# Four groups of residual transposes at the end of an output projection gathered into one group, one product pair later

## The chip, the cores and the metric

One core of one Trainium2 chip runs the whole kernel. The metric is device microseconds for one execution. The kernel before takes 525.51 us (median of 3 runs, 525.22 to 525.74). Traces and engine names: PE is TensorE's matrix product, PEld its loading of the stationary operand, DVE is VectorE, ACT is ScalarE, POOL is GpSimd, SP is SyncE.

## The reference

One layer of an encoder on a residual `x` of 512 positions by 1024, in fp32:

```
h = RMSNorm(x);  [xr|gate|q|k|v] = h @ W_in
y_rnn  = (rg_lru_fwd(conv(xr)) + rg_lru_bwd(conv(xr))) * gelu(gate)
y_attn = dilated_attention(q, k, v)
x = x + concat(RMSNorm(y_rnn), RMSNorm(y_attn)) @ W_out
h = RMSNorm(x)
x = x + relu(h @ W_up)^2 @ W_down
out = RMSNorm(x)
```

The change lies where `x + ... @ W_out` ends and `h @ W_up` begins. The up projection needs the new residual with the model dimension on the partitions, so the residual is transposed there.

## The kernel before, in words

**Products.** Each fp32 operand is split into a high part and a low part (an ACT copy gives the high part, a DVE subtraction the low one). `mm3` (L311) then issues three products for one tile: high by high (L312), high by low (L313), low by high (L314). The first argument of `mm3` is the stationary operand. Weight chunks of 128x1024 are streamed: `conv_hi(i)` (L240) makes `whi` of chunk `i` on ACT, `conv_lo(i)` (L261, the subtraction at L269) makes `wlo` on DVE. Both run about three chunks ahead of PE.

**Order.** On PE, ACT, DVE and POOL the program order written in the kernel is the order of execution (`tc.manual_schedule`, L107). Nothing is moved behind another by a planner on these four engines. SP's queue of loads is planned outside the attention part.

**End of the output projection.** The attention half of `W_out` is multiplied as seven block products (`OSEQ`, L62: 11, s2, s3, s4, 21, s1, 22), each of four pairs `i` = 0 to 3, where pair `i` is `tt, k = i // 2, i % 2` (L1259 to L1266). One pair is one `mm3`. After `k == 1` the DVE instruction of `wo_x` (L1202, recorded at L1208) adds the product to the residual and writes a quarter of `x1n`. Block s1 writes `x1n[2,1]` and `x1n[3,1]`; block 22 writes `x1n[0,1]` and `x1n[1,1]`; so the right half of the new residual is complete only after the last pair of 22. The left half (`x1n[*,0]`) comes from blocks 21 and s4. What else is issued after each pair stands in the table `BES` (L1248 to L1258).

**Transposes.** `h2_t(k, tag)` (L1211) handles column block `k` of the residual: four PE transposes of 128x128 into one PSUM bank named `pxt` (L1218), then two ACT copies out of it: `h2h` (L1219) and `hm` (L1221). `h2_l(k)` (L1224) makes `h2l` on DVE. Blocks 0 to 3 read the left half and are spread over the pairs of s1 and 22, one group of four transposes each. Blocks 4 to 7 read the right half and are issued together, 16 transposes, after `k == 0` of the first three tiles of the up projection (L1531 to L1541). `pxt` uses the PSUM tags `gs` and `et`, two banks each; blocks 0 to 3 use `gs` only.

**Up projection, first three tiles.** For `k` = 0 to 7 and `i` = 0 to 2, PE multiplies chunk `c0 + i` by `h2h[k]`, `h2l[k]` into `pu`. The chunks are `C_WA+7`, `C_WA+8` and `C_WA+9`; their `conv_lo` stand in `BES` (after pair 3 of 21, pair 3 of s1 and pair 2 of 22).

The lines that the change and the prediction touch are `BES["s1"]` and `BES["22"]` (L1257, L1258), `h2_t` (L1211), `h2_l` (L1223), `wo_x` (L1202) and the start of the up projection (L1529 to L1541):

```
for k in range(KD):
    if k == 1:
        for j in range(4, 8):
            h2_t(j, "gs" if j < 6 else "et")
            h2_l(j)
    for i in range(start):
        mm3(pu[i], wk(c0 + i, k), h2k(k), k == 0, k == KD - 1)
```

Of the kernel before, what the change touches and what calls it, by code (L numbers as in the profile page):

```python
# [98 lines left out]
def hybrid_kernel(ctx: ExitStack, tc, xw0, xw, xn, w_in, w_v, w_out, w_up, w_dn, gates, vecs, bias, fg, out):  # L99
# [13 lines left out]
    def g_(name, dt=FT, shape=(P, S)):  # L113
        return work.tile(list(shape), dt, name=name, tag="g", bufs=NG)
# [4 lines left out]
    def ps_(name, tag):  # L119
        return psum.tile([P, S], FT, name=name, tag=tag, bufs={"pj": 4, "gs": 2, "et": 2}[tag])  # L120

    def f(t):
        return t.bitcast(FT)
# [4 lines left out]
    def vec(n, i):  # L128
        return vt[:, VEC[n] + i:VEC[n] + i + 1]
# [74 lines left out]
    C_G, C_V, C_QK, C_WO, C_WA, C_UP = 4, 8, 12, 20, 24, 31  # L204
# [3 lines left out]
    def ublock(h, b, f):  # L208
        return w_up[h * HF + f + {"11": 0, "12": 1, "21": 2, "22": 3}[b]]
# [11 lines left out]
    def wblock(h, b, q):  # L221
        return w_dn[h, int(b[1]) - 1, (int(b[0]) - 1) * NQ + q]
# [3 lines left out]
    def emit_dma():  # L226
        if plain:
            i = plain.popleft()
            r = stream.tile([P, 1024], FT, name="wraw", tag="wraw", bufs=3)
            nc.sync.dma_start(r, source(chunks[i]))  # L230
            raws[i] = r
# [29 lines left out]
    def conv_lo(i):  # L261
        if i < len(chunks):
            i = swap.get(i, i)
            r = raws.pop(i)
            if i in remade:
                splits[i] += (remade.pop(i),)
                return
            lo = stream.tile([P, 1024], FR, name="wlo", tag="wlo", bufs=4)
            nc.vector.tensor_tensor(lo, r, f(splits[i][0]), op=OP.subtract)  # L269
            splits[i] += (lo,)  # L270
            c = chunks[i]
            if isinstance(c, tuple) and c[0] == "o":
                return
            if isinstance(c, tuple) and len(c) == 4:
                h, kind, f0 = c[:3]
                if kind == "t1" and cq[h, f0, "t2"] not in raws:
                    nc.gpsimd.dma_start(r, ublock(h, "22", f0), accum_op=OP.add)
                    raws[cq[h, f0, "t2"]] = r
                elif kind == "22":
                    t = raws[cq[h, f0, "t3"]]  # L280
                    nc.vector.tensor_tensor(t, t, r, op=OP.add)
                elif kind in ("t2", "21"):
                    held[kind] = r
                    if len(held) == 2:
                        t = held.pop("t2")
                        nc.vector.tensor_tensor(t, t, held.pop("21"), op=OP.add)
                        raws[cq[h, f0, "t4"]] = t
                        emit_dma()
                if kind in ("11", "22"):
                    emit_dma()  # L290
            elif isinstance(c, tuple) and c[1][0] == "s":
                nxt = {"s1": ("s2", "22"), "s2": ("s4", "21")}.get(c[1])
                if nxt:
                    nc.gpsimd.dma_start(r, wblock(c[0], nxt[1], c[2]), accum_op=OP.add)
                    raws[cd_[c[0]] + {"s2": 2 * NQ + 2 * c[2], "s4": 6 * NQ + c[2]}[nxt[0]]] = r
            elif i not in (C_WO + 2, C_WO + 3):
                emit_dma()
# [492 lines left out]
    et, en, zs = {}, {}, {}  # L790
# [103 lines left out]
    def o_src(n, k):  # L894
        return at[k][:, tl] if n == "11" else osum[n, k]
# [4 lines left out]
    def o_lo(n, k):  # L900
        hi, lo = osp[n]
        c = slice(k * TH, (k + 1) * TH)
        nc.vector.tensor_tensor(lo[:, c], o_src(n, k), f(hi)[:, c], op=OP.subtract)
# [307 lines left out]
    def h2_t(k, tag):  # L1211
        if not hb:
            hb["h"] = big.tile([P, KD, S], FR, name="h2h", tag="bigB")
            hb["l"] = [t[:, j, :] for c in ("bigC", "bigD") for t in (big.tile([P, KD // 2, S], FR, name="h2l", tag=c),) for j in range(KD // 2)]
        pt = ps_("pxt", tag)
        n, j = k // 4, k % 4
        for tt in range(4):
            nc.tensor.transpose(pt[:, tt * P:(tt + 1) * P], x1n[tt, n][:, j * P:(j + 1) * P], ident)  # L1218
        act(hb["h"][:, k, :], pt, AF.Copy, scale=vec("mg", k))  # L1219
        hm[k] = g_("hm")  # L1220
        act(hm[k], pt, AF.Copy, scale=vec("mg", k))  # L1221

    def h2_l(k):  # L1223
        nc.vector.tensor_tensor(hb["l"][k], hm[k], f(hb["h"])[:, k, :], op=OP.subtract)  # L1224
# [20 lines left out]
    def cv(j):  # L1245
        return {0: lambda: conv_hi(C_WA + j), 3: lambda: conv_lo(C_WA + j)}

    BES = {w: cv(i + 3) for i, w in enumerate(OSEQ)}  # L1248
# [5 lines left out]
    BES["s3"][3] = lambda: (conv_lo(C_WA + 5), st["wo"](3))  # L1254
    BES["s4"].update({1: lambda: (o_lo("s1", 0), o_sum("22", 1)), 2: lambda: o_hi("22", 1)})
    BES["21"].update({1: lambda: o_lo("s1", 1), 3: lambda: conv_lo(C_WA + 7)})
    BES["s1"].update({1: lambda: (o_lo("22", 0), o_lo("22", 1), h2_t(0, "gs")), 2: lambda: h2_t(1, "gs"), 3: lambda: (conv_lo(C_WA + 8), h2_l(0))})  # L1257
    BES["22"].update({1: lambda: (h2_t(2, "gs"), h2_l(1)), 2: lambda: (h2_t(3, "gs"), conv_lo(C_WA + 9)), 3: lambda: (h2_l(2), h2_l(3))})  # L1258
    for w in OSEQ:  # L1259
        for i in range(4):  # L1260
            tt, k = i // 2, i % 2
# [260 lines left out]
    for half in range(2):  # L1522
# [6 lines left out]
        if half == 0:  # L1529
            start = 3  # L1530
            pu = [ps_("pu", "pj") for _ in range(start)]  # L1531
# [7 lines that stand above are left out]
                    if i == 0:  # L1539
                        feed(c0, k)  # L1540
                if k in (2, 3, 4, 5):  # L1541
                    h_sums(k - 2)
                if k == 6:
                    x1_sq(0, 0)
                if k in (5, 7):
                    h_hi("t1", k // 7)
                    h_lo("t1", k // 7)
            conv_hi(c0 + 4)
            conv_lo(c0 + 4)
            for i in (0, 1):  # L1550
                up_evac(i, pu[i])
            conv_hi(c0 + 5)
            conv_lo(c0 + 5)
            up_evac(2, pu[2])
# [262 lines left out]
```

## Time and profile before

| what | value |
|---|---|
| time, median of 3 runs | 525.51 us (525.22 to 525.74) |
| profiled execution, span from first to last instruction | 523.7 us, 8216 instructions |
| profiled execution's own time | the page gives its span only; the median lies 1.8 us above that span |
| PE busy | 517.1 us (99%), 3021 products |
| DVE busy | 430.4 us (82%) |
| ACT busy | 352.2 us (67%) |
| chain that ended last | PE 99% |
| mean granted TensorE clock | 0.999 |

A busy time of PE includes modelled ends of pipelined products, so a product is shown with 0.39 us where the next one starts 0.23 us later. The chain of waits removes that overlap: there each product of 512 columns counts 0.23 us. The timeline merges neighbouring instructions of one kind into one row; its bracket gives the idle time of the engine before the instruction and what ended it.

### The profile page before, as it was taken

What the parts mean: (1) busy time and instruction counts of PE and PEld (TensorE: products, weight loads), DVE (VectorE), ACT (ScalarE), POOL (GpSimd) and SP (SyncE); (2) the same over time, 40 slices, a digit from 0 to 9 for tenths busy, and PEclk for the clock granted to TensorE, in tenths of its full rate; (3) what the DMA queues carried; (4) which work ended last, traced back from release to release, by engine and by line L of the source; (5) the groups of instructions that cost most, each with busy time, mean ns of one, the idle gap of its engine ahead of it and who ended that gap; (6) DMA issues with size and microseconds to landing.
All of it is one profiled execution on the core that took longest, in us unless ns stands there. A gap on an engine that the chain in (4) does not pass through costs nothing.

```text
span 523.7 us, 8216 instructions
## 1 busy us (share of the span) xinstructions
PE 517.1 (99%) x3021; PEld 444.3 (85%) x3021; DVE 430.4 (82%) x668; ACT 352.2 (67%) x570; POOL 65.3 (12%) x89
## 2 busy tenths in 40 slices
PE   9999999999999999999999999999999999999995
PEld 8867888778777788899999888889999999888884
DVE  6899986788886898898789987789766978986885
ACT  7579946667857857586578666565667577655655
POOL 0173000000000321001300312001100300131000
PEclk9999999999999999999999999999999999999999
DMA  7636555266796499947595899976986497799704
GB/s 288 208 99 196 161 160 180 83 191 199 190 294 197 115 196 247 353 134 195 139 223 143 213 273 281 306 271 161 300 256 168 117 224 210 157 289 257 195 1 161
DMA packets 40329, 105.15 MB, mean 201 GB/s; under 512 B 5056, under 2 KB 13376, under 8 KB 40288
## 3 DMA queue, kind: packets, MB, share of 16 engines
q1 hardware_dynamic: 32448, 78.10, 44.5%
q0 software_dynamic: 7696, 26.32, 27.3%
q8 instruction: 24, 0.39, 0.3%
q10 hardware_dynamic: 144, 0.20, 0.1%
q14 instruction: 17, 0.14, 0.1%
HBM read 95.59 MB, written 4.29 MB: 191 GB/s over the span
## 4 chain that ended last, share of the span: by engine, by line
PE 99%; DVE 0%; issue 0%; DVEq 0%; ACT 0%; ACTq 0%
PE pu L314 10%; PE pu L312 10%; PE pu L313 10%; PE pd L314 10%; PE pd L312 10%; PE pd L313 10%; PE pqk L312 3%; PE pqk L314 3%; PE pqk L313 3%; PE pwo L312 3%; PE pwo L314 3%; PE pwo L313 3%; PE pav L942 2%; PE pt L842 2%; PE ps L806 2%; PE pp L312 1%
## 5 line engine op out<-in xcount | busy, mean ns | idle before, releaser
L269 DVE TENSOR_TENSOR wlo<-wraw,whi 128x1024 fp32r<-128x1024 f32 x71 | 86.6, 1220 | 24.0 <-ACT whi L247 23.9
L247 ACT ACTIVATE whi<-wraw 128x1024 fp32r<-128x1024 f32 x67 | 70.8, 1057 | 37.4 <-PE pd L314 18.4
L313 PE MATMUL pd<-wlo,ah 128*128 128x512 f32 (+1 forms) x195 | 75.2, 386 | 0.0
L312 PE MATMUL pd<-whi,ah 128*128 128x512 f32 (+1 forms) x195 | 75.2, 386 | 0.0
L314 PE MATMUL pd<-whi,al 128*128 128x512 f32 (+1 forms) x195 | 75.2, 386 | 0.0
L313 PE MATMUL pu<-hl,whi 128*128 128x256 f32 x224 | 63.4, 283 | 0.0
L314 PE MATMUL pu<-hh,wlo 128*128 128x256 f32 x224 | 63.4, 283 | 0.0
L312 PE MATMUL pu<-hh,whi 128*128 128x256 f32 x224 | 63.4, 283 | 0.0
L312 PE MATMUL pu<-h2h,whi 128*128 128x256 f32 (+1 forms) x200 | 60.1, 300 | 0.0
L313 PE MATMUL pu<-h2l,whi 128*128 128x256 f32 (+1 forms) x200 | 60.0, 300 | 0.0
L314 PE MATMUL pu<-h2h,wlo 128*128 128x256 f32 (+1 forms) x200 | 60.0, 300 | 0.0
L269 DVE TENSOR_TENSOR wlo<-tw,whi 128x1024 fp32r<-128x1024 f32 x37 | 45.2, 1221 | 17.7 <-ACT whi L247 17.7
L247 ACT ACTIVATE whi<-tw 128x1024 fp32r<-128x1024 f32 x38 | 40.1, 1058 | 24.9 <-PE pd L314 6.3
L312 PEld LDWEIGHTS pu<-hh,whi 128*128 128x128 f32 x224 | 43.0, 192 | 0.0
L313 PEld LDWEIGHTS pu<-hl,whi 128*128 128x128 f32 x224 | 43.0, 192 | 0.0
L314 PEld LDWEIGHTS pu<-hh,wlo 128*128 128x128 f32 x224 | 43.0, 192 | 0.0
L313 PEld LDWEIGHTS pd<-wlo,ah 128*128 128x128 f32 x195 | 36.6, 188 | 7.4
L312 PEld LDWEIGHTS pd<-whi,ah 128*128 128x128 f32 x195 | 36.6, 188 | 7.3
L314 PEld LDWEIGHTS pd<-whi,al 128*128 128x128 f32 x195 | 36.6, 188 | 7.4
L247 ACT ACTIVATE whi<-ts 128x1024 fp32r<-128x1024 f32 x24 | 25.4, 1060 | 25.2 <-PE pd L314 16.4
L313 PEld LDWEIGHTS pu<-h2l,whi 128*128 128x128 f32 x200 | 38.3, 191 | 1.3
L314 PEld LDWEIGHTS pu<-h2h,wlo 128*128 128x128 f32 x200 | 38.3, 191 | 1.3
(280 smaller groups left out, 1220.1 us busy)
## 6 DMA issues: line engine op xcount, KB each, us to landing
wraw<-in_w_up_dram SPq DMA_DIRECT2D x25, 512.0 KB, 4.8
ts<-in_w_dn_dram POOLq DMA_DIRECT2D x24, 512.0 KB, 13.5
wraw<-in_w_dn_dram SPq DMA_DIRECT2D x24, 512.0 KB, 8.7
tw<-in_w_up_dram SPq DMA_DIRECT2D x15, 512.0 KB, 6.7
tw<-in_w_up_dram POOLq DMA_DIRECT2D x15, 512.0 KB, 7.5
wraw<-in_w_in_dram SPq DMA_DIRECT2D x13, 512.0 KB, 4.3
ts<-in_w_dn_dram SPq DMA_DIRECT2D x8, 512.0 KB, 9.0
tw<-in_w_dn_dram SPq DMA_DIRECT2D x8, 512.0 KB, 7.0
```

Of the source, the lines that this page charges most:

```text
L247: act(hi, raws[i], AF.Copy)
L269: nc.vector.tensor_tensor(lo, r, f(splits[i][0]), op=OP.subtract)
L312: nc.tensor.matmul(o, lhsT=a[0], rhs=b[0], start=bool(first), stop=False, skip_group_check=on)
L313: nc.tensor.matmul(o, lhsT=a[0], rhs=b[1], start=False, stop=False, skip_group_check=on)
L314: nc.tensor.matmul(o, lhsT=a[1], rhs=b[0], start=False, stop=bool(last), skip_group_check=on)
L806: nc.tensor.matmul(psq[p, u][e][:, :NK], lhsT=qs_[p, a][r, P * qt:P * qt + P], rhs=kks[p][r, b, w:w + NK], start=i == 0, stop=i == 2)
L842: nc.tensor.transpose(pt[:, i * P:(i + 1) * P], en[h][qt][:, k:k + P], ident)
L942: nc.tensor.matmul(pav[p][a, co], lhsT=vs[:, jt, h * DH:(h + 1) * DH], rhs=et[h, jt][:, ci], start=jt == 0 and i == 0, stop=jt == 3 and i ...
```

## The change

The body of `h2_t` is cut into a PE part (`h2_pe`, the four transposes) and an ACT part (`h2_ev`, the two copies). In the table `BES`, the four groups of transposes that stood after pair 1 of s1, pair 2 of s1, pair 1 of 22 and pair 2 of 22 become one group of 16 after pair 2 of s1. Blocks 0 and 1 stay in the tag `gs`; blocks 2 and 3 take the tag `et`, so that the group has four PSUM banks. The copies of blocks 0 and 1 stand in ACT's order after pair 2 of s1, those of blocks 2 and 3 keep their places after pairs 1 and 2 of 22. The order of DVE's instructions is not changed.

```
+        h2_pe(k, tag)
+        h2_ev(k)
+    pxt = {}
+    def h2_pe(k, tag):
+        pt = pxt[k] = ps_("pxt", tag)
         n, j = k // 4, k % 4
         for tt in range(4):
             nc.tensor.transpose(pt[:, tt * P:(tt + 1) * P], x1n[tt, n][:, j * P:(j + 1) * P], ident)
+    def h2_ev(k):
+        pt = pxt.pop(k)
         act(hb["h"][:, k, :], pt, AF.Copy, scale=vec("mg", k))
         hm[k] = g_("hm")
         act(hm[k], pt, AF.Copy, scale=vec("mg", k))
...
-    BES["s1"].update({1: lambda: (o_lo("22", 0), o_lo("22", 1), h2_t(0, "gs")), 2: lambda: h2_t(1, "gs"), 3: lambda: (conv_lo(C_WA + 8), h2_l(0))})
-    BES["22"].update({1: lambda: (h2_t(2, "gs"), h2_l(1)), 2: lambda: (h2_t(3, "gs"), conv_lo(C_WA + 9)), 3: lambda: (h2_l(2), h2_l(3))})
+    BES["s1"].update({1: lambda: (o_lo("22", 0), o_lo("22", 1)), 2: lambda: (h2_t(0, "gs"), h2_t(1, "gs"), h2_pe(2, "et"), h2_pe(3, "et")), 3: lambda: (conv_lo(C_WA + 8), h2_l(0))})
+    BES["22"].update({1: lambda: (h2_ev(2), h2_l(1)), 2: lambda: (h2_ev(3), conv_lo(C_WA + 9)), 3: lambda: (h2_l(2), h2_l(3))})
```

## Rows read from the trace of the kernel before

**Rows 1.** The page, part 1: busy time, share of the span, instructions.

```profile
PE 517.1 (99%) x3021; PEld 444.3 (85%) x3021; DVE 430.4 (82%) x668; ACT 352.2 (67%) x570; POOL 65.3 (12%) x89
```

**Rows 2.** Chain that ended last, from 205 us to the end: shares by line.

```profile
by line: PE pu L314 16.8%; PE pu L312 16.8%; PE pu L313 16.8%; PE pd L314 15.9%; PE pd L312 15.8%; PE pd L313 15.8%; DVE x1n L1482 0.2%; DVE x1n L1473 0.2%; DVE scr L1483 0.1%; DVE x1n L1475 0.1%; DVE tw L1493 0.1%; issue 0.1%; DVEq L1813 0
```

**Rows 3.** Waits from 192 to 212 us: engine, line, releaser: total us, times, longest.

```profile
DVE h2l L1224 <- ACT hm L1221: 2.1, 4, 0.7
...
DVE x1n L1208 <- PE pwo L314: 0.3, 1, 0.3
PEld pxt L1218 <- DVE x1n L1208: 0.2, 1, 0.2
```

**Rows 4.** Chain that ended last, 194 to 204 us: start, us, what.

```profile
194.50 0.24 PE pwo L314
194.73 0.44 PE pxt L1218 x4
...
196.77 0.24 PE pwo L314
...
199.53 0.44 PE pxt L1218 x4
...
200.43 0.23 PE pwo L314
...
202.49 0.23 PE pu L314
202.71 1.79 PE pxt L1218 x16
```

**Rows 5.** Timeline of DVE, 195 to 203 us: start, us, instruction [idle before].

```profile
195.99 0.75 DVE L903 TENSOR_TENSOR ol<-osum,oh 128x256 fp32r<-128x256 f32 x2
197.05 0.75 DVE L1208 SCALAR_TENSOR_TENSOR x1n<-pwo,nrc,x 128x512 f32<-128x512 f32 x1 [0.31 <-PE pwo L314]
197.71 1.21 DVE L269 TENSOR_TENSOR wlo<-wraw,whi 128x1024 fp32r<-128x1024 f32 x1
198.85 0.69 DVE L1224 TENSOR_TENSOR h2l<-hm,h2h 128x512 fp32r<-128x512 f32 x1
...
200.71 1.22 DVE L269 TENSOR_TENSOR wlo<-wraw,whi 128x1024 fp32r<-128x1024 f32 x1
201.84 0.74 DVE L1208 SCALAR_TENSOR_TENSOR x1n<-pwo,nrc,x 128x512 f32<-128x512 f32 x1
```

**Rows 6.** Timeline of PEld, 200 to 205 us.

```profile
200.50 0.19 PEld L313 LDWEIGHTS pu<-h2l,whi 128*128 128x128 f32 x1
...
202.10 0.19 PEld L314 LDWEIGHTS pu<-h2h,wlo 128*128 128x128 f32 x1
202.33 0.14 PEld L1218 LDWEIGHTS pxt<-ident,x1n 128*128 128x128 f32 x1
202.64 1.62 PEld L1218 LDWEIGHTS pxt<-ident,x1n 128*128 128x128 f32 x15 [0.17 <-DVE x1n L1208]
204.23 0.19 PEld L312 LDWEIGHTS pu<-h2h,whi 128*128 128x128 f32 x1
```

**Rows 7.** Timeline of ACT, 195 to 199 us.

```profile
195.21 0.69 ACT L1219 ACTIVATE h2h<-pxt,vt 128x512 fp32r<-128x512 f32 x1 [0.69 <-PE pxt L1218]
...
197.50 1.08 ACT L247 ACTIVATE whi<-wraw 128x1024 fp32r<-128x1024 f32 x1
```

**Rows 8.** Chain that ended last, in the attention: groups of six transposes.

```profile
117.98 0.81 PE pt L842 x6
121.53 0.66 PE pt L842 x6
```

**Rows 9.** Busy time by stretch: us, PE, PEld, DVE, ACT, POOL (instructions), PEclk, DMA share, GB/s.

```profile
201.00:203.00 2.00, 2.00 (x12) 1.59 (x11) 2.00 (x3) 0.29 (x1) 0.00 (x0) 1.00 1.03 219
...
518.00:520.00 2.00, 0.00 (x0) 0.00 (x0) 1.85 (x8) 0.96 (x3) 0.00 (x0) 1.00 0.59 151
520.00:523.70 3.70, 0.00 (x0) 0.00 (x0) 0.19 (x1) 0.13 (x1) 0.00 (x0) 0.81 0.40 142
```

More of the change, by code (lines that the diff above doesn't have):

```diff
@@ L1214, in h2_t @@
             hb["l"] = [t[:, j, :] for c in ("bigC", "bigD") for t in (big.tile([P, KD // 2, S], FR, name="h2l", tag=c),) for j in range(KD // 2)]
-        pt = ps_("pxt", tag)
+        h2_pe(k, tag)
[3 more added lines that the diff above has]
+        pt = pxt[k] = ps_("pxt", tag)
         n, j = k // 4, k % 4
```

## The prediction, made before the changed kernel was run

> **What bounds the kernel now.** I read the busy times first. TensorE is busy 99% of the span [rows 1], so a microsecond added to PE anywhere is a microsecond of the result unless PE waits later for something else. The chain from 205 us to the end answers that: it consists of the products of `pu` and `pd` and a last piece of DVE work of about 1% [rows 2]. No wait of PE is left there that could swallow a delay, so what the stage around the change gains or loses reaches the end in full. The question is thus only when PE comes out of that stage.
>
> Then I read the waits of the stage. Two count. VectorE waits 0.31 us for a product before one `x1n` instruction, and PE's loader waits 0.17 us for another `x1n` [rows 3, 5, 6]. The timeline of DVE shows that these two belong together. At 197.05 DVE begins `x1n[3,1]`, which had to wait for pair 3 of block s1 (the product at 196.77 of [rows 4]). From there DVE runs without a gap: `wlo` of `C_WA+8`, `h2l[0]`, `x1n[0,1]`, `h2l[1]`, `wlo` of `C_WA+9` and `x1n[1,1]`, which ends at 201.84 + 0.74 = 202.58 [rows 5]. The second of PE's 16 transposes loads at 202.64, 0.06 after that [rows 6]. So in this stage DVE is the bound: PE -> `x1n[3,1]` -> six DVE instructions back to back -> PE. PE arrives at the second transpose only slightly too early.
>
> **The change part by part: the groups.** Removed: four groups of four transposes, 0.44 us each (the first and the last of four are shown) [rows 4], 1.76 together. Added: one group of 16. The trace has such a group, blocks 4 to 7, with 1.79 us in the chain [rows 4], but that holds the wait. Without it: 15 loads go from 202.64 to the next product's load at 204.23 [rows 6], 1.59 / 15 = 0.106 each, so 16 take 1.70. Bounds: 1.62 (1.79 less the whole 0.17), and 2.16 at the dearest transposes of the trace (0.81 / 6 = 0.135 each; the cheap kind of the same group is 0.66 / 6 = 0.11) [rows 8]. I take 1.70, since it is the same instruction with the same tiles. PE alone would therefore win 1.76 - 1.70 = 0.06 us. A group pays nearly nothing for being a group of its own: 0.11 per transpose in a group of four, 0.106 in one of 16.
>
> **The place.** Before, two groups (0.88) lay ahead of the end of s1's pair 3: one after pair 1, one after pair 2. After the change the whole group of 16 does: 1.70. So pair 3 of s1 ends 1.70 - 0.88 = 0.82 later. DVE was already waiting there: its work before it ends at 195.99 + 0.75 = 196.74 [rows 5], so no slack is left, and `x1n[3,1]` begins at 197.05 + 0.82 = 197.87. The wait of DVE grows from 0.31 to about 1.13. Behind it in DVE's order stand the six instructions named above. None of them is moved by the diff, and each was started as the last one ended, so all slip by 0.82: `h2l[0]` ends at 198.85 + 0.69 + 0.82 = 200.36, `wlo` of `C_WA+9` at 200.71 + 1.22 + 0.82 = 202.75, `x1n[1,1]` at 203.40.
>
> **Who waits for them.** After pair 3 of s1, PE has no transposes left in block 22, so it makes the 0.88 of the two later groups good and reaches the up projection at -0.06 against before. There:
> - `h2l[0]` is needed at the load at 200.50 - 0.06 = 200.44 [rows 6], 0.08 after its end. Just in time; a few hundredths late would be covered by the next two.
> - `wlo` of `C_WA+9` is needed by the last product of `k == 0`, whose load stood at 202.10 [rows 6], now 202.04. It is there at 202.75 plus 0.06: a wait of about 0.75 that the trace of before does not have.
> - `x1n[1,1]` is needed by the second transpose of block 4. Before, that loaded at 202.64; now it can at 202.64 + 0.82 = 203.46.
>
> The last two do not add up. From the load of that product to the load of the second transpose PE needs about 0.45 (202.10 to 202.64 less the 0.09 that the wait cost beyond the usual spacing), and DVE takes 0.65 from the end of `wlo` to the end of `x1n[1,1]`; so the later one decides. PE leaves the stage 0.82 later than before, although its own work shrank by 0.06.
>
> **What costs nothing.** ACT's copies of block 0 begin 0.68 later, one pair (195.21 to about 195.9) [rows 7]; the four copies of blocks 0 and 1 push `whi` of `C_WA+9` from 197.50 to about 198.2, where it takes 1.08, and it is wanted by DVE at 200.71 + 0.82 = 201.5 and by PE at about 201.6 (two products before the load at 202.10). That is a cover of over 2 us. Copies of blocks 2 and 3 don't wait for PE any more; `h2h[2]` is wanted after the second set of transposes only. The new banks (`et`) were last read by `wo_x` of s4, two blocks of products earlier; blocks 6 and 7 take them again near 204, after the copies. Loads on SP follow `conv_lo` and slip with it by 0.8 us, three chunks ahead of their use. If that cover were gone it would show as a wait of PE, of which there is none after 205 now [rows 2].
>
> **Sum.** 0.82 on a span of 523.7 gives 524.5. The median of the runs lies 1.8 above the profiled span, so 525.51 + 0.82 = 526.3 us. With the group at 1.62 it is +0.74 (526.25), at 2.16 it is +1.28 (526.8).
>
> [...] The granted clock is 1.00 in the stretch with the group of 16 and its wait, and stays 1.00 from 518 to 520 us, where PE does nothing; only the last 3.7 us show 0.81 [rows 9]. [...]
>
> **Rivals.** *A gain.* If DVE made up the delay, the 0.06 of PE and the 0.09 of the old wait remain: -0.06 to -0.15, 525.4. For it: PE is the bound of the whole, and the group's work does shrink. Against it: the chain of DVE has no gap from 197.05 to 202.58, and `x1n[3,1]` already waits for PE [rows 5]. It would need 0.8 us of idle DVE in that stretch. [...]
>
> *Slower beyond doubt.* The group of 16 that now lies ahead of DVE's wait costs as much per transpose as the dear groups of the attention, 0.135 instead of 0.106 [rows 8]. Then pair 3 of s1 is 2.16 - 0.88 = 1.28 late, and 526.8 comes out. For it: the group switches to banks of another tag and ACT reads two of them meanwhile. Against it: the group of 16 in the same stage had the same mixture. It decides (over 0.2%, 1.05 us) from a group of 1.93 us on.
>
> [...]
>
> **How the numbers follow.** The forecast, DVE's chain slipping by 0.82, gets 0.73; the gain 0.09; the dear group 0.15; the clock 0.03. A difference of 0.2% (1.05 us) is about what a measurement of this kernel can tell from no change. The forecast's +0.82 is inside it, with about 0.04 of its own chance beyond; with the two slow rivals that makes 0.21 slower. The gain is inside it too, and only 0.02 is left for faster. Same: 0.77. The range goes from 525.5 (taking in part of the gain) to 526.9 (the dear group).
>
> **What would show it.** DVE's wait before `x1n[3,1]` at 1.0 to 1.2 us instead of 0.31; no wait among the six that follow; a new wait of PE's loader for `wlo` of about 0.7 us and one for `x1n` of 0.2 to 0.5; the 16 transposes of blocks 4 to 7 beginning their second load near 203.5; everything after that later by the same 0.8. The first group of 16 in the chain with 1.7. I am wrong if PE's loader shows no wait there, if the group of 16 is far from 1.7, or if the 0.8 is given back before the end.

## The result, and the profile after

The changed kernel takes 525.91 us (median of 21 runs, 525.37 to 526.43) against 525.22 for the kernel before in the same sessions (21 runs, 524.64 to 525.98). The medians differ by 0.69 us. The ratio is 1.0015, with a 95% interval of 1.001 to 1.0021: on 525.22 that is slower by 0.79 us, between 0.53 and 1.10.

The profiled span is 524.0 us, with 525.76 for that execution, against 523.7 before. That difference of 0.3 is not the loss: the stage began 0.56 us earlier in the profile after (pair 1 of s1 ends at 194.17, before at 194.73). Nearly all of that arises at the very start of the kernel, which the change doesn't touch: in the chain, nine PE instructions that write `pxr` (L453, from 4.52 us on) take 3.35 us in the profile before and 2.82 in the one after. So stages are compared here and not spans. I measure the stage from the end of pair 1 of s1 to the end of the second set of 16 transposes, both in the chain that ended last. Before it runs from 194.73 to 202.71 + 1.79 = 204.50 [rows 4], 9.77 us.

The chain of the changed kernel over the same stretch (start, us, what):

```profile
193.94 0.23 PE pwo L314
...
194.62 0.23 PE pwo L314
194.86 1.75 PE pxt L1224 x16
...
197.06 0.25 PE pwo L314
197.31 0.03 issue
197.34 0.04 DVE x1n L1208
...
198.01 0.75 DVE wlo L269
...
199.14 0.68 DVE h2l L1233
199.82 0.66 DVE x1n L1208
200.48 0.60 DVE h2l L1233
201.08 1.14 DVE wlo L269
202.22 0.67 DVE x1n L1208
202.89 0.04 issue
202.93 1.86 PE pxt L1224 x15
```

The stage goes from 193.94 + 0.23 = 194.17 to 202.93 + 1.86 = 204.79: 10.62 us, 0.85 more. What the reader is to see is that the chain leaves PE here. Before, it ran through products and transposes alone [rows 4]. Now it goes over to DVE with `x1n[3,1]` at 197.34 and comes back to PE only at 202.93, with the six DVE instructions that the prediction named. The rest of the kernel is unchanged: 523.7 - 204.50 = 319.2 before, 524.0 - 204.79 = 319.2 after.

The waits of the changed kernel from 192 to 213 us (engine, line, releaser: total us, times, longest) answer to [rows 3]:

```profile
DVE x1n L1208 <- PE pwo L314: 1.2, 1, 1.2
PEld pu L314 <- DVE wlo L269: 0.8, 1, 0.8
PE pu L314 <- DVE wlo L269: 0.4, 1, 0.4
PEld pxt L1224 <- DVE x1n L1208: 0.4, 1, 0.4
```

DVE's wait grew from 0.3 to 1.2, PE's loader has a wait for `wlo` that was not there, and its wait for `x1n` doubled.

The timeline of DVE after, answering to [rows 5]:

```profile
195.43 0.75 DVE L903 TENSOR_TENSOR ol<-osum,oh 128x256 fp32r<-128x256 f32 x2
197.34 0.75 DVE L1208 SCALAR_TENSOR_TENSOR x1n<-pwo,nrc,x 128x512 f32<-128x512 f32 x1 [1.16 <-PE pwo L314]
198.01 1.21 DVE L269 TENSOR_TENSOR wlo<-wraw,whi 128x1024 fp32r<-128x1024 f32 x1
199.14 0.68 DVE L1233 TENSOR_TENSOR h2l<-hm,h2h 128x512 fp32r<-128x512 f32 x1
199.74 0.74 DVE L1208 SCALAR_TENSOR_TENSOR x1n<-pwo,nrc,x 128x512 f32<-128x512 f32 x1
200.40 0.68 DVE L1233 TENSOR_TENSOR h2l<-hm,h2h 128x512 fp32r<-128x512 f32 x1
201.00 1.22 DVE L269 TENSOR_TENSOR wlo<-wraw,whi 128x1024 fp32r<-128x1024 f32 x1
202.14 0.74 DVE L1208 SCALAR_TENSOR_TENSOR x1n<-pwo,nrc,x 128x512 f32<-128x512 f32 x1
```

The two rows of before that [rows 5] leaves out, for the comparison:

```profile
199.45 0.74 DVE L1208 SCALAR_TENSOR_TENSOR x1n<-pwo,nrc,x 128x512 f32<-128x512 f32 x1
200.11 0.68 DVE L1224 TENSOR_TENSOR h2l<-hm,h2h 128x512 fp32r<-128x512 f32 x1
```

One wait in front, then no bracket until the last row, before as after: counted from the end of pair 1 of s1, `x1n[3,1]` begins 0.85 us later (3.17 for 2.32) and `x1n[1,1]` ends 0.86 later (8.71 for 7.85). The timeline of PE's loader, answering to [rows 6], shows where it arrives:

```profile
202.27 0.19 PEld L314 LDWEIGHTS pu<-h2h,wlo 128*128 128x128 f32 x1 [0.83 <-DVE wlo L269]
202.40 0.14 PEld L1224 LDWEIGHTS pxt<-ident,x1n 128*128 128x128 f32 x1
202.93 1.62 PEld L1224 LDWEIGHTS pxt<-ident,x1n 128*128 128x128 f32 x15 [0.39 <-DVE x1n L1208]
```

`wlo` ends on DVE at 201.00 + 1.22 = 202.22 and its load begins at 202.27; `x1n[1,1]` ends at 202.88 and the load of the second transpose begins at 202.93.

The clock stayed up through both waits and the transposes (us, PE, PEld, DVE, ACT, POOL, then PEclk, DMA share, GB/s):

```profile
201.00:203.00 2.00, 1.55 (x7) 0.72 (x6) 2.00 (x4) 0.03 (x1) 0.00 (x0) 1.00 1.07 225
203.00:205.00 2.00, 2.00 (x17) 1.96 (x18) 1.26 (x3) 1.48 (x3) 0.00 (x0) 1.00 1.03 272
```

### The profile page after: what moved, and what is told of

Read it like the earlier page. It is cut to its first block, busy times and chain, and to the rows that moved or that the text cites. A ratio compares the mean times of both kernels' runs of the same rounds, so it can differ in the third digit from the quotient of the medians.

```text
span 524.0 us, 8214 instructions
## 1 busy us (share of the span) xinstructions
PE 516.9 (99%) x3021; PEld 444.0 (85%) x3021; DVE 430.3 (82%) x668; ACT 352.3 (67%) x570; POOL 65.4 (12%) x89
## 4 chain that ended last, share of the span: by engine, by line
PE 97%; DVE 1%; issue 0%; DVEq 0%; ACT 0%; ACTq 0%
PE pu L313 10%; PE pu L314 10%; PE pu L312 10%; PE pd L313 10%; PE pd L312 10%; PE pd L314 10%; PE pqk L312 3%; PE pqk L314 3%; PE pqk L313 3%; PE pwo L312 3%; PE pwo L314 2%; PE pwo L313 2%; PE pav L942 2%; PE pt L842 2%; PE ps L806 2%; PE pp L312 1%
## 5 line engine op out<-in xcount | busy, mean ns | idle before, releaser
L312 PEld LDWEIGHTS pu<-h2h,whi 128*128 128x128 f32 x200 | 38.3, 191 | 1.3
```

The lines of the kernel that those rows point to most:

```text
L312: nc.tensor.matmul(o, lhsT=a[0], rhs=b[0], start=bool(first), stop=False, skip_group_check=on)
```

## The experiments

All six start from the changed kernel and move one or two entries of the table `BES`. DVE's order is that of the changed kernel except in the third and fourth; the order on ACT is the same in all.

| kernel | transposes ahead of pair 3 of s1 | stage, from and to | stage, us | against before | ratio to before, 95% interval |
|---|---|---|---|---|---|
| before | 8 | 194.73, 204.50 | 9.77 | | |
| changed | 16 | 194.17, 204.79 | 10.62 | +0.85 | 1.0015, 1.001 to 1.0021 |
| group after pair 3 | 0 | 195.00, 204.67 | 9.67 | -0.10 | 1.0, 0.9991 to 1.0009 |
| group after pair 1 | 16 | 195.03, 205.66 | 10.63 | +0.86 | 1.0019, 1.001 to 1.0028 |
| `wlo` of `C_WA+8` first | 16 | 194.23, 203.90 | 9.67 | -0.10 | 1.0001, 0.999 to 1.0012 |
| `wlo` of `C_WA+9` last | 16 | 194.59, 205.60 | 11.01 | +1.24 | 1.0024, 1.0015 to 1.0034 |
| 8 and 8 | 8 | 194.58, 204.32 | 9.74 | -0.03 | 0.9985, 0.9969 to 1.0001 |
| 12 and 4 | 12 | 194.12, 204.30 | 10.18 | +0.41 | 1.0009, 0.9995 to 1.0024 |

The stage of each is taken from its chain as above. By the times alone, three kernels are slower than before (the changed one, the group after pair 1, `wlo` of `C_WA+9` last) and the others can't be told from it, 12 and 4 included. The stages in the traces carry the finer differences, from one profile each; two pairs of kernels that should have the same stage agree to 0.01 (10.62 and 10.63, 9.67 and 9.67).

**The group after pair 3.** The same group of 16, the same four banks, one pair later still:

```
-  1: lambda: (o_lo("22", 0), o_lo("22", 1)), 2: lambda: (h2_t(0, "gs"), h2_t(1, "gs"), h2_pe(2, "et"), h2_pe(3, "et")), 3: lambda: (conv_lo(C_WA + 8), h2_l(0))
+  1: lambda: (o_lo("22", 0), o_lo("22", 1)), 3: lambda: (h2_t(0, "gs"), h2_t(1, "gs"), h2_pe(2, "et"), h2_pe(3, "et"), conv_lo(C_WA + 8), h2_l(0))
```

> The same group of 16 in the same four banks, issued after pair 3 of s1 instead of after pair 2; all else as in the changed kernel. Theory (VectorE's chain from x1n[3,1] to x1n[1,1] decides when TensorE resumes): VectorE's wait of 1.16 us before x1n[3,1] goes, the chain starts about 1.1 us earlier, no wait for wlo or x1n is left at TensorE, and the stage is shorter by the old loss of 0.85 plus the 0.15 of group and wait that the first kernel still had: about -1.0 us against the changed kernel, 524.9, or -0.1 to -0.2 against the kernel before. Rival (the group itself is dear: 16 in a row, the second pair of banks, copies beside it): the loss stays, 525.9.

Measured: 524.8 us (median of 11) beside 524.97 of before in the same session. The chain of this kernel:

```profile
196.13 0.24 PE pwo L314
196.37 1.75 PE pxt L1224 x16
...
202.69 0.23 PE pu L314
202.92 1.75 PE pxt L1224 x16
```

and its DVE:

```profile
196.26 0.74 DVE L903 TENSOR_TENSOR ol<-osum,oh 128x256 fp32r<-128x256 f32 x2
196.93 0.74 DVE L1208 SCALAR_TENSOR_TENSOR x1n<-pwo,nrc,x 128x512 f32<-128x512 f32 x1
```

No bracket stands before `x1n[3,1]`, the chain never leaves PE, and the stage is 0.95 shorter than in the changed kernel. The group and its banks are thus free of the loss; the rival that put it there is out.

**The group after pair 1.** One pair earlier than in the changed kernel, so that the group begins where the first group of before began:

```
-  1: lambda: (o_lo("22", 0), o_lo("22", 1)), 2: lambda: (h2_t(0, "gs"), h2_t(1, "gs"), h2_pe(2, "et"), h2_pe(3, "et"))
+  1: lambda: (o_lo("22", 0), o_lo("22", 1), h2_t(0, "gs"), h2_t(1, "gs"), h2_pe(2, "et"), h2_pe(3, "et"))
```

> The same group of 16 after pair 1 of s1, one pair earlier than in the changed kernel, so that pair 2 and pair 3 follow it. Theory: 16 transposes still lie ahead of pair 3, so x1n[3,1] is as late as before, and the time is that of the changed kernel within 0.1 us (525.9); VectorE waits 1.1 to 1.2 us before x1n[3,1], TensorE again for wlo. Rival (it is the move by one pair that costs, since the copies and what follows them start 0.68 us later): 0.4 to 0.7 us come back, 525.2 to 525.5.

Measured: 525.73 us beside 524.97, and a stage of 10.63. The wait in DVE's timeline is that of the changed kernel:

```profile
198.21 0.75 DVE L1208 SCALAR_TENSOR_TENSOR x1n<-pwo,nrc,x 128x512 f32<-128x512 f32 x1 [1.17 <-PE pwo L314]
```

So "one product pair later" is not what costs. It is also only a part of the change: of the four groups of before, the first came one pair later and the second stayed, while the third and the fourth came three and four pairs earlier, ahead of pair 3 of s1. What matters is how many transposes lie ahead of that pair.

**`wlo` of `C_WA+8` first.** Nothing on PE is moved; one DVE instruction changes its place (and with it the loads on SP that follow `conv_lo`; the kernel with the group after pair 3 has the same stage without that):

```
-  2: lambda: (h2_t(0, "gs"), h2_t(1, "gs"), h2_pe(2, "et"), h2_pe(3, "et")), 3: lambda: (conv_lo(C_WA + 8), h2_l(0))
+  2: lambda: (h2_t(0, "gs"), h2_t(1, "gs"), h2_pe(2, "et"), h2_pe(3, "et"), conv_lo(C_WA + 8)), 3: lambda: h2_l(0)
```

> TensorE's and ScalarE's order exactly as in the changed kernel; only VectorE's wlo of C_WA+8 (1.21 us) is issued ahead of x1n[3,1] instead of behind it, into the time in which VectorE waits. Theory: the chain behind x1n[3,1] is 1.14 us shorter, both waits of TensorE go, about -1.0 us against the changed kernel (524.9). Rival (the group of 16 or its banks cost the 0.8 on TensorE itself): no change, 525.9.

Measured: 524.79 us beside 524.97, stage 9.67. In its chain PE works through without a wait:

```profile
194.00 0.23 PE pwo L314
...
194.91 1.75 PE pxt L1224 x16
...
202.15 1.75 PE pxt L1224 x16
```

Its DVE:

```profile
196.16 1.21 DVE L269 TENSOR_TENSOR wlo<-wraw,whi 128x1024 fp32r<-128x1024 f32 x1
197.39 0.75 DVE L1208 SCALAR_TENSOR_TENSOR x1n<-pwo,nrc,x 128x512 f32<-128x512 f32 x1
198.06 0.68 DVE L1233 TENSOR_TENSOR h2l<-hm,h2h 128x512 fp32r<-128x512 f32 x1
```

The 1.21 us fill the time in which DVE waited, and the whole loss is gone with TensorE's order untouched. This is the direct test of the chain: shortening it by one instruction on DVE gives back what the transposes on PE seemed to cost.

**`wlo` of `C_WA+9` last.** The order of the two instructions that PE waits for is turned round:

```
-  2: lambda: (h2_ev(3), conv_lo(C_WA + 9)), 3: lambda: (h2_l(2), h2_l(3))
+  2: lambda: h2_ev(3), 3: lambda: (conv_lo(C_WA + 9), h2_l(2), h2_l(3))
```

> As the changed kernel, but VectorE makes wlo of C_WA+9 after x1n[1,1] instead of before it. Theory (the two waits of TensorE lie in a row on its path, and in the changed kernel only the later one counts): x1n[1,1] ends 1.1 us earlier, wlo 0.7 later (near 202.9 on the changed kernel's clock); TensorE's loader waits for wlo until then and has another 0.45 us to go to the second transpose: +0.45 to +0.55 us against the changed kernel, 526.4. Rival (only x1n[1,1] holds TensorE): -0.7 us, 525.2.

Measured: 526.34 us beside 524.97, stage 11.01, which is 0.39 more than the changed kernel. The loads on SP that follow `conv_lo` moved by one place with it. Its waits from 192 to 213 us:

```profile
PEld pu L314 <- DVE wlo L269: 1.5, 1, 1.5
DVE x1n L1208 <- PE pwo L314: 1.2, 1, 1.2
PE pu L314 <- DVE wlo L269: 1.1, 1, 1.1
```

The wait for `x1n` is gone from PE and the wait for `wlo` has grown. PE meets the two waits one behind the other, so what counts is whichever lets it go later: in the changed kernel `x1n[1,1]`, here `wlo`. `x1n[1,1]` alone doesn't hold PE: the rival had 0.7 us less, the run has 0.4 more. The chain shows the way from `wlo` to the transposes:

```profile
202.16 1.14 DVE wlo L269
203.30 0.04 issue
203.35 0.51 PE pu L314
203.85 1.75 PE pxt L1224 x16
```

The size was a little off, 0.39 for an expected 0.45 to 0.55. PE had 0.55 to go from the end of `wlo` to the transposes; but the 16 then took 1.75, where in the changed kernel the last 15, behind their wait, took 1.86.

**Eight and eight, twelve and four.** The group is split around pair 3:

```
-  2: lambda: (h2_t(0, "gs"), h2_t(1, "gs"), h2_pe(2, "et"), h2_pe(3, "et")), 3: lambda: (conv_lo(C_WA + 8), h2_l(0))
+  2: lambda: (h2_t(0, "gs"), h2_t(1, "gs")), 3: lambda: (h2_pe(2, "et"), h2_pe(3, "et"), conv_lo(C_WA + 8), h2_l(0))      # 8 and 8
+  2: lambda: (h2_t(0, "gs"), h2_t(1, "gs"), h2_pe(2, "et")), 3: lambda: (h2_pe(3, "et"), conv_lo(C_WA + 8), h2_l(0))      # 12 and 4
```

> Eight of the 16 transposes after pair 2 of s1, the other eight after pair 3; banks, copies and VectorE's order as in the changed kernel. Theory: eight lie ahead of pair 3, as many as in the kernel before, so VectorE waits about 0.3 us before x1n[3,1], TensorE's wait for wlo goes, and the stage (end of pair 1 of s1 to the end of the second set of 16) has the 9.7 to 9.8 us of the kernel before: about -0.85 us against the changed kernel, same as before. Rival (the larger group or the second pair of banks costs a part of the 0.8): a part of the loss stays, at least 0.2.

> Twelve transposes after pair 2 of s1, four after pair 3. Theory: the loss goes by the number of transposes ahead of pair 3, 0.44 for four: VectorE waits about 0.7 us, the stage is 0.4 to 0.45 us longer than with eight ahead, 10.2 us, half the way to the changed kernel's 10.62. Rival (a threshold: the wait for wlo makes the loss, all or nothing): 9.7 or 10.6.

Measured: 524.86 us for 8 and 8, 525.69 for 12 and 4, beside 525.24 of before. Neither ratio is clear of no change, and the two medians lie 0.83 apart where the stages lie 0.44 apart; so the amount in between rests on the traces. The stages are 9.74 and 10.18. The two rows of DVE, first of 8 and 8, then of 12 and 4:

```profile
196.87 0.75 DVE L1208 SCALAR_TENSOR_TENSOR x1n<-pwo,nrc,x 128x512 f32<-128x512 f32 x1 [0.28 <-PE pwo L314]
```

```profile
196.85 0.75 DVE L1208 SCALAR_TENSOR_TENSOR x1n<-pwo,nrc,x 128x512 f32<-128x512 f32 x1 [0.73 <-PE pwo L314]
```

The wait before `x1n[3,1]` is none with 0 transposes ahead, 0.28 with 8, 0.73 with 12, 1.16 with 16. The stage follows with 9.67, 9.74, 10.18 and 10.62: 0.44 for every four transposes beyond eight. Between none and eight there is only 0.07: with none no wait holds PE (above), with eight its loader waits 0.2 us for `x1n`, as before [rows 3]. No kernel with four was run. With twelve the stage lies half way, and not at 9.7 or 10.6, as the rival of a threshold had it.

## Why the prediction was right

**What bounds the stage.** Right. PE is busy 99% of the span, and yet in this stage the path runs through DVE. The third experiment shows it without touching PE.

**The groups.** The forecast let PE win 0.06 by having one group instead of four. In the transposes it wins 0.01: the group of 16 takes 1.75 (in the changed kernel, and twice where nothing waits in the kernel with the group after pair 3), not 1.70, and four groups of four took 1.76. My 0.106 per transpose came from loads after a wait; the unhindered price is 1.75 / 16 = 0.109. So the term was 0.05 too small, and with 1.75 the sum would have been 1.75 - 0.88 = 0.87 against a measured 0.85. By another way a win of about that size is there, which is luck: where no wait holds PE, the stage is 0.10 shorter than before. Of this 0.04 is the old wait (1.79 before, 1.75 without it), 0.01 the transposes, and 0.05 lies in the 27 products of the stage (9.77 - 1.76 - 1.79 = 6.22 before, 9.67 - 1.75 - 1.75 = 6.17). Why they are shorter stays open, and there is one profile of before.

**The place.** Right: `x1n[3,1]` waits 0.85 us longer (1.16 for 0.31; about 1.13 was forecast), and the six instructions behind it slip without a gap.

**Who waits.** Right. `h2l[0]` caused no wait. The loader waited 0.83 for `wlo` (about 0.75 forecast) and 0.39 for `x1n` (0.2 to 0.5). That the two don't add up and the later one decides stands by the fourth experiment: with `wlo` last, PE waits for `wlo` alone, and the loss is 1.24.

**What costs nothing.** Right: 319.2 us remain after the stage in every kernel of the table (span less the end of the stage), so nothing that follows gave the loss back or added to it.

**Sum.** 0.82 forecast, 0.85 in the stage, 0.79 by the ratio (0.53 to 1.10). The time is 525.91 and not 526.3 mostly because the kernel before ran at 525.22 in the 21 runs beside it, 0.29 below the three runs on which the forecast stood; the rest is that the medians differ by 0.69 and not by 0.82. Two things in the chances were off. The prediction took 1.05 us as about the least that can be told from no change, while 21 runs of each kernel told 0.79. And its parts of a clear loss, 0.04, 0.15 and 0.03, make 0.22 and not 0.21.

**Rivals.** The gain did not come: DVE had no idle time from 197.34 to 202.88 to make up the delay, and the gathering was worth the 0.06 of transposes and products above, at most. The dear group is out with 1.75. No run shows a lower granted clock in this stretch, to which the chances give 0.03: in the changed kernel it was 1.00 from 201 to 205 us, through the waits and the transposes, and in the chain of every kernel the products of `k == 1` behind them took 0.23 to 0.24 us each.

A version that beats both kernels clearly was not found. The kernels with the group after pair 3 or with `wlo` of `C_WA+8` first have a stage 0.10 shorter than before; their times can't be told from the kernel before.

## What to carry to other kernels

An engine that is busy 99% of the span can still be released by another one in a given stage: before moving work on it, look for the small wait of the other engine (0.31 us here) and count what stands without a gap between that wait and the first engine's next wait. Here eight more transposes (0.87 us) ahead of the product that ends this wait made the stage 0.85 longer, while all 16 behind it cost nothing (9.67 us for 9.77). And a delay of that kind can be undone on the waiting engine, by moving a piece of its independent work into the wait: one `wlo` of 1.21 us took the stage from 10.62 to 9.67.

## What the runs showed of the hardware

Transposes of 128x128 between the products of this stage, where they wait for nothing, cost 0.109 to 0.11 us each whether they come in fours (0.44), eights (0.87), twelves (1.31) or sixteens (1.75): three groups fewer saved 0.01 in the transposes and, by one profile of before, 0.05 in the products beside them. And the start of the stage moves by up to 0.9 us between profiles of kernels that do the same up to there (pair 1 of s1 ends at 194.12 in one and at 195.03 in another), which is as much as the whole effect: spans of single profiles would have ranked these kernels wrongly.
